# A hybrid decoder layer on one core: the opening takes two column chunks in turn, and its first loads come from two queues

## The chip, the core and the metric

The kernel runs on one core of a Trainium2 chip. TensorE (PE in the rows) multiplies, VectorE (DVE) and ScalarE (ACT) prepare operands and evacuate results, GpSimd (POOL) does a few tiny operations, and SyncE (SP) issues the loads, which the core's 16 DMA engines carry out. The metric is the device time of one execution in microseconds (us).

## The reference

One decoder layer on 256 tokens of width 1024, all in float32:

```
h = rms_norm(x, g_pre_mix);  proj = h @ w_in          # 1024 -> 3072: q, k, v of attention; q, k, v, gate of retention
x = x + rms_norm(concat(moba(...), retention(...)) @ w_out)
x = x + rms_norm(cross_attention(rms_norm(x), rms_norm(mem)) @ w_co)
x = x + rms_norm((silu(gate) * up) @ w_down)
```

## The kernel before

All weights come as one stream of 130 blocks of 128 x 1024 float32 (512 KB), in the order of use. A block q holds two k tiles (128 rows each) of 512 columns. `load_weight(q)` (line 120) issues its load from SyncE into one of five `raw` buffers, so the load of block q + 5 waits until block q has been split. `split_weight(q)` (line 125) splits it exactly into a high and a low part `hl` of type float32r: ScalarE copies the high part (line 131), VectorE subtracts to get the low part (line 132). `x`, transposed, is split in the same way into `xT`, one k tile (128 x 256) at a time, with the norm's gain multiplied in (`gain_split`, line 151: ScalarE line 154, VectorE line 155). A product of x and w is three passes: high x high, high x low, low x high. So a block costs TensorE 2 k tiles x 3 passes x 2 token tiles (`t`, 128 tokens each) = 12 matmuls of 512 columns.

TensorE's program is a list of steps, written once in Python (`steps`, `col_steps`, line 612). The first stage is the product with `w_in`, in six column chunks of 512; a chunk needs 4 blocks, one for each pair of k tiles, and accumulates in two PSUM banks, one per token tile. Between the steps, the Python code also emits the weight splits, a few blocks ahead, and the side work (rotation, attention, norms), which runs on the other engines and now and then puts small matmuls into TensorE's queue. The table `WAIT` holds by how many steps each part of the side work is delayed. Every engine runs its own queue strictly in the order in which the code emitted it.

The opening (from line 709): eight matmuls on zeros (`warm`, line 715), then the loads of x (`xg`: gains and k tile 0; `xr0`: k tiles 1 to 3; `xr1`: 4 to 7) and of blocks 0 to 4 (`raw0` in two halves of 256 KB), taken in turn, all from SyncE. Block 0 is taken half by half: the step `first` (line 817) goes over both token tiles in each of the three passes. From block 1 on the step `col` does all of token tile 0, and then token tile 1. Every loaded pair of k tiles of x has to be split on ScalarE and VectorE before the block that uses it.

```
for kk in range(2):
    steps.append(("first", 0, kk))
    steps.append(("none", 0))
for c in range(6):
    col_steps(plain([c]), both, in_done, "xT")
...
opening = {0: lambda: x_split(2), 1: lambda: x_split(3)}
late = {WAIT["xd"]: x_load, WAIT["xs"]: x_stats, WAIT["ms"]: mem_stats}
```

Of the kernel before, what the change touches and what calls it, by code (L numbers as in the profile page):

```python
# [14 lines left out]
P = 128  # L15
# [8 lines left out]
# main steps between the parts of the side work, and the pace of the weight splits  # L24
# [8 lines left out]
}  # L33
WARM = 8

# [4 lines left out]
def tile_hybrid_layer(  # L40
# [11 lines left out]
    """weights is one stream of 130 [128, 1024] blocks in the order of use.  Each float32 block is  # L52
    split exactly into hi + lo float32r parts; a product takes three float32r passes
    (hi*hi + hi*lo + lo*hi).  Tokens are the stationary operand, weights the moving one."""
# [53 lines left out]
    def need(*keys):  # L108
        """the producers of these parts have been emitted"""
        missing = [k for k in keys if k not in emitted]  # L110
        assert not missing, missing
# [56 lines left out]
    def row_rms(key):  # L168
        """1/rms of each token along the free axis, the same on all partitions."""
        T[f"R_{key}"] = cpool.tile([P, 256], F32, tag="R", name=f"R_{key}")  # L170
        c = accC(f"c_R_{key}")
        for t in range(2):
            nc.tensor.transpose(c[:, t, :], rstd[f"{key}{t}"][:, 0:1].to_broadcast([P, P]), ident)
        nc.scalar.activation(T[f"R_{key}"], c[:, 0:2, :].rearrange("p t k -> p (t k)"), AF.Copy)
# [44 lines left out]
    def softmax_unit(key, n, keys, scale, fill, row=None, finish=None):  # L219
        """fill(s) emits the scores of n heads into two banks; leaves the transposed probabilities in pt_key."""  # L220
# [41 lines left out]
    def moba_unit(t, g):  # L262
        keys = P * (t + 1)
        n = D // keys
        hn = n // 2

        def fill(s):
            """even heads in one bank, odd heads in the other; the contraction is over half of the rows"""
            need(f"q{t}", *[f"k{u}" for u in range(t + 1)])
            for i in range(hn):  # L270
                j = g * hn + i
                for e in range(2):
                    rows = slice(64 * e, 64 * e + 64)
                    nc.tensor.matmul(s[e][:, i * keys:(i + 1) * keys], T["qT"][rows, j, tok(t)],  # L274
                                     T["kT"][rows, j, 0:keys], start=(i == 0), stop=False, skip_group_check=True)
            for e in range(2):
                nc.tensor.matmul(s[e].rearrange("p (h k) -> p h k", h=hn)[:, :, keys - P:keys], identb,
                                 maskb[:, None, :].to_broadcast([P, hn, P]), start=False, stop=True,
                                 skip_group_check=True)
            yield 0  # L280

        return softmax_unit(f"m{t}{g}", n, keys, 0.125, fill)
# [46 lines left out]
    def ret_scores():  # L329
        """key block 0 against all queries, then key block 1 against query block 1"""  # L330
# [107 lines left out]
    def tri(dst, a, b, start, stop):  # L438
        """dst (+)= a.T @ b from the (hi, lo) parts of both"""
# [8 lines left out]
    def half_tiles(name):  # L448
        """[P, 8, 256] in two parts of four"""
# [163 lines left out]
    def col_steps(order, tiles, done, st):  # L613
        """order: list of (chunk, k pair); tiles: token tile order; one block of the stream each."""
# [6 lines left out]
        for i, t in seqs:  # L621
# [3 lines left out]
            if base + i == 0:  # L625
                continue
            steps.append(("col", base + i, t, st, kp, (c, t), s == 0, s + 1 == count[c], done))

    def row_steps(order, done, st):
        """like col_steps, but with the weights stationary: the result is transposed, two 128-wide  # L630
        column blocks of all 256 tokens per accumulator."""
# [16 lines left out]
    for kk in range(2):  # L648
        steps.append(("first", 0, kk))
        steps.append(("none", 0))  # L650
    for c in range(6):
# [58 lines left out]
    nc.vector.memset(junk[:, 0:512], 0.0)  # L710
    nc.gpsimd.memset(mhalf, -0.5)
    nc.scalar.preload_act_table(AF.Exp)
# [14 lines left out]
    raws[0] = rawp.tile([P, D], F32, tag="raw", name="raw0")  # L727
    for kk in range(2):
        nc.sync.dma_start(xg if kk == 0 else xr[0][:, 1, :], gx[:, 0:288] if kk == 0 else gx[:, 288:544])
        nc.sync.dma_start(raws[0][:, kk * 512:(kk + 1) * 512], weights[0, :, kk * 512:(kk + 1) * 512])  # L730
    for q in range(1, RAW):
        if q < 4:
            nc.sync.dma_start(xr[q // 2][:, 2 * (q % 2):2 * (q % 2) + 2, :],
                              gx[:, 32 + 512 * q:544 + 512 * q].rearrange("p (k m) -> p k m", k=2))
        load_weight(q)
# [48 lines left out]
    for kk in range(2):  # L784
        n = slice(kk * 512, (kk + 1) * 512)
        gain_split("xT", 0, xg[:, 32:288] if kk == 0 else xr[0][:, 1, :], kk)
        if kk == 0:
            nc.vector.tensor_copy(hls[0][:, 0, n], raw[:, n])
        else:
            nc.scalar.activation(hls[0][:, 0, n], raw[:, n], AF.Copy)  # L790
        nc.vector.tensor_tensor(out=hls[0][:, 1, n], in0=raw[:, n], in1=hls[0][:, 0, n].bitcast(F32), op=ALU.subtract)
    load_weight(RAW)
    x_split(1)
    split_weight(1, 2)
    opening = {0: lambda: x_split(2), 1: lambda: x_split(3)}
# [4 lines left out]
    for i, s in enumerate(steps):  # L800
# [17 lines left out]
        if s[0] == "first":  # L818
            kk = s[2]
            h = hls[0][:, :, kk * 512:(kk + 1) * 512]  # L820
            for a, (hx, hw) in enumerate(((0, 0), (1, 0), (0, 1))):
                for t in range(2):
                    if i == 0 and a == 0:
                        accs[(0, t)] = accS(f"acc{t}")
                    nc.tensor.matmul(accs[(0, t)], T["xT"][:, hx, kk, tok(t)], h[:, hw, :], start=(kk == 0 and a == 0),
# [77 lines left out]
def _layout(inputs):  # L903
# [11 lines left out]
    for c in (0, 1, 3, 4, 5, 2):  # L915
# [80 lines left out]
```

## Time and profile before

| | |
|---|---|
| median of 3 runs | 415.37 us (414.7 to 415.68) |
| profiled execution, first to last instruction | 415.7 us |
| mean granted TensorE clock in it | 0.994 of full speed |
| TensorE busy with matmuls | 405.9 us (98%), 2530 matmuls |
| VectorE / ScalarE / GpSimd busy | 261.0 / 219.8 / 11.0 us |
| bytes moved, mean rate | 76.23 MB, 183 GB/s |

The profiled execution's own time is its span, 415.7 us; the profile records nothing outside it. It lies 0.3 us above the median of the runs, and at the upper end of their range. Times in the rows are counted from the span's start. An engine is busy while an instruction of it runs; a wait is put down to what ended it.

### The profile page before, as it was taken

To read this page: it belongs to the slowest core of one execution; us is meant where nothing else is said; L and a number is where in the kernel's file an instruction comes from. 1 tells how busy PE (TensorE), PEld (TensorE's weight loads), DVE (VectorE), ACT (ScalarE), POOL (GpSimd) and SP (SyncE) were. 2 spreads that over 40 slices of the span, in tenths; PEclk is the share of its full clock that TensorE was granted. 3 is DMA by queue.
4 is the path that set the end of the run, shared out by engine and by line. 5 is a ranking of instruction groups with operands and counts; after the bars stand their busy time and mean duration, and the time that the engine had idled before them with its cause. 6 is when DMAs were issued, how large, how long until landed. Compare 5 with 4: busy or idle time off the path is not lost.

```text
span 415.7 us, 6402 instructions
## 1 busy us (share of the span) xinstructions
PE 405.9 (98%) x2530; PEld 359.6 (87%) x2530; DVE 261.0 (63%) x356; ACT 219.8 (53%) x360; POOL 11.0 (3%) x21
## 2 busy tenths in 40 slices
PE   6999999999999999999999999999999999999994
PEld 3788887888899999988888889989989989998983
DVE  4866875666848884576547867664674665566332
ACT  4956965945836673484346765352453443434111
POOL 0010010100010000000011000000000000000000
PEclk9899999999999999999999999999999999999999
DMA  7986846574645666135406777657447348353002
GB/s 247 417 322 215 297 131 224 151 247 155 190 169 178 224 248 213 52 101 202 153 0 203 239 246 271 207 188 211 160 158 245 122 145 291 106 203 102 0 21 82
DMA packets 21774, 76.23 MB, mean 183 GB/s; under 512 B 2416, under 2 KB 2672, under 8 KB 21744
## 3 DMA queue, kind: packets, MB, share of 16 engines
q1 hardware_dynamic: 21744, 75.82, 53.8%
q8 instruction: 20, 0.33, 0.3%
q14 instruction: 10, 0.08, 0.1%
HBM read 74.76 MB, written 1.05 MB: 182 GB/s over the span
## 4 chain that ended last, share of the span: by engine, by line
PE 94%; issue 2%; DMA 2%; SPq 1%; ACT 0%; DVE 0%; DVEq 0%; POOLq 0%; POOL 0%
PE acc L838 12%; PE acc L839 12%; PE acc L840 12%; PE acc L861 12%; PE acc L860 12%; PE acc L858 12%; PE down L881 4%; PE down L882 4%; PE down L880 4%; DMA raw<-in_weights_dram 2%; PE s_m L274 1%; PE o_m L303 1%; PE pt_m L253 1%; PE ro L356 0%; PE xt_cross L422 0%
## 5 line engine op out<-in xcount | busy, mean ns | idle before, releaser
L132 DVE TENSOR_TENSOR hl<-raw,hl 128x1024 fp32r<-128x1024 f32 (+1 forms) x132 | 154.1, 1198 | 49.4 <-ACT hl L131 49.1
L131 ACT ACTIVATE hl<-raw 128x1024 fp32r<-128x1024 f32 (+1 forms) x132 | 131.8, 1038 | 39.9 <-PE acc L861 15.0
L858 PE MATMUL acc<-x2T,hl 128*128 128x256 f32 x288 | 81.6, 283 | 0.0
L861 PE MATMUL acc<-x2T,hl 128*128 128x256 f32 x288 | 81.5, 283 | 0.0
L860 PE MATMUL acc<-x2T,hl 128*128 128x256 f32 x288 | 81.5, 283 | 0.0
L860 PEld LDWEIGHTS acc<-x2T,hl 128*128 128x128 f32 x288 | 55.3, 192 | 0.2
L858 PEld LDWEIGHTS acc<-x2T,hl 128*128 128x128 f32 x288 | 55.3, 192 | 0.2
L861 PEld LDWEIGHTS acc<-x2T,hl 128*128 128x128 f32 x288 | 55.3, 192 | 0.0
L838 PE MATMUL acc<-hl,xT 128*128 128x512 f32 x92 | 38.1, 414 | 1.7 <-ACT hl L131 1.7
L839 PE MATMUL acc<-hl,xT 128*128 128x512 f32 x92 | 36.6, 398 | 0.2 <-DVE hl L132 0.2
L840 PE MATMUL acc<-hl,xT 128*128 128x512 f32 x92 | 36.7, 399 | 0.0
L880 PE MATMUL down<-hl,fT 128*128 128x512 f32 x88 | 34.3, 390 | 0.0
L881 PE MATMUL down<-hl,fT 128*128 128x512 f32 x88 | 34.3, 390 | 0.0
L882 PE MATMUL down<-hl,fT 128*128 128x512 f32 x88 | 34.2, 389 | 0.0
L838 PEld LDWEIGHTS acc<-hl,xT 128*128 128x128 f32 x92 | 17.7, 193 | 5.8 <-ACT hl L131 2.1
L839 PEld LDWEIGHTS acc<-hl,xT 128*128 128x128 f32 x92 | 17.8, 193 | 3.8 <-DVE hl L132 0.5
L840 PEld LDWEIGHTS acc<-hl,xT 128*128 128x128 f32 x92 | 17.6, 191 | 3.8
L882 PEld LDWEIGHTS down<-hl,fT 128*128 128x128 f32 x88 | 16.5, 188 | 3.4
L880 PEld LDWEIGHTS down<-hl,fT 128*128 128x128 f32 x88 | 16.5, 188 | 3.3
L881 PEld LDWEIGHTS down<-hl,fT 128*128 128x128 f32 x88 | 16.5, 188 | 3.3
L510 ACT ACTIVATE sg<-sg 128x512 f32<-128x512 f32 x9 | 5.7, 633 | 24.9 <-DVE sg L509 24.9
L858 PE MATMUL acc<-memT,hl 128*128 128x256 f32 x64 | 18.4, 287 | 0.0
(207 smaller groups left out, 721.8 us busy)
## 6 DMA issues: line engine op xcount, KB each, us to landing
raw<-in_weights_dram SPq DMA_DIRECT2D x129, 512.0 KB, 4.4
gpost<-in_gpost_dram SPq DMA_DIRECT2D x3, 512.0 KB, 5.0
x_sb<-in_x_dram SPq DMA_DIRECT2D x2, 512.0 KB, 7.0
memn<-in_mem_dram SPq DMA_DIRECT2D x2, 512.0 KB, 6.1
mr<-in_memT_dram SPq DMA_DIRECT2D x2, 512.0 KB, 5.1
out_dram<-x_sb SPq DMA_DIRECT2D x4, 256.0 KB, 2.0
xr<-in_gx_dram SPq DMA_DIRECT2D x3, 256.0 KB, 6.5
raw<-in_weights_dram SPq DMA_DIRECT2D x2, 256.0 KB, 3.3
```

Of the source, the lines that this page charges most:

```text
L131: nc.scalar.activation(h[:, 0, n], raw[:, n], AF.Copy)
L132: nc.vector.tensor_tensor(out=h[:, 1, n], in0=raw[:, n], in1=h[:, 0, n].bitcast(F32), op=ALU.subtract)
L510: nc.scalar.activation(sg, sg, AF.Silu)
L838: nc.tensor.matmul(acc, xh, h[:, 0, kk, :], start=(first and kk == 0), stop=False)
L839: nc.tensor.matmul(acc, xh, h[:, 1, kk, :], start=False, stop=False)
L840: nc.tensor.matmul(acc, xl, h[:, 0, kk, :], start=False, stop=(last and kk == 1))
L858: nc.tensor.matmul(dst, h[:, 0, kk, n], xh, start=(first and b == 0 and kk == 0), stop=False, skip_group_check=True)
L860: nc.tensor.matmul(dst, h[:, 0, kk, n], xl, start=False, stop=False, skip_group_check=True)
L861: nc.tensor.matmul(dst, h[:, 1, kk, n], xh, start=False, stop=(last and kk == 1), skip_group_check=True)
L880: nc.tensor.matmul(acc, fh, wh, start=first, stop=False, skip_group_check=True)
L881: nc.tensor.matmul(acc, fh, wl, start=False, stop=False, skip_group_check=True)
L882: nc.tensor.matmul(acc, fl, wh, start=False, stop=last, skip_group_check=True)
```

## The change

1. The first two chunks of columns, 0 and 1, are taken in turn: for each pair of k tiles first the block of chunk 0, then that of chunk 1. The stream of weights is laid out in this order (blocks 0 to 7). Before, it was all four pairs for chunk 0, then all four for chunk 1.
2. Blocks 0 to 3 (`EARLY = 4`), not block 0 alone, use the step `first`, which goes over both token tiles in each pass. The accumulators of both chunks are then four banks of the pool `psS`.
3. The first half of block 0 is loaded from ScalarE's queue, ahead of its table load; the other loads stay on SyncE, without the strict alternation: block 1 is now ahead of k tiles 2 and 3, blocks 2 and 3 ahead of k tiles 4 to 7, which come as one load.
4. The splits of x stand later: those of k tiles 2 and 3 behind the split of block 1, those of 4, 5 and of 6, 7 behind the splits of blocks 4 and 6. For the first half of block 0 VectorE copies the weights before it makes the low part of x.
5. Five entries of `WAIT` change (`mq` from 2 to 0, `rope_q0` from 8 to 4, `rope_q1` from 9 to 5, `xd` from 0 to 3, `xs` from 8 to 12): the load of x in its natural layout, its statistics and the evacuation of the queries are emitted at other steps.

Comment lines that the change removes are left out here.

```
-    7, "rope_q0": 8, "rope_q1": 9, "rope_r0": 3, "rope_r1": 9, "rs": 1, "rsc": 12, "sc_c0": 0, "sc_c1": 1,
+    7, "rope_q0": 4, "rope_q1": 5, "rope_r0": 3, "rope_r1": 9, "rs": 1, "rsc": 12, "sc_c0": 0, "sc_c1": 1,
...
+EARLY = 4
...
-    for kk in range(2):
-        steps.append(("first", 0, kk))
-        steps.append(("none", 0))
-    for c in range(6):
+    early = [(c, kp) for kp in range(4) for c in (0, 1)]
+    for q in range(EARLY):
+        for kk in range(2):
+            steps.append(("first", q, kk, *early[q]))
+            if q == 0:
+                steps.append(("none", 0))
+    col_steps(early, both, in_done, "xT", EARLY)
+    for c in range(2, 6):
         col_steps(plain([c]), both, in_done, "xT")
...
+    raws[0] = rawp.tile([P, D], F32, tag="raw", name="raw0")
+    nc.scalar.dma_start(raws[0][:, 0:512], weights[0, :, 0:512])
     nc.scalar.preload_act_table(AF.Exp)
...
     load_weight(RAW)
+    split_weight(1, 2)
     x_split(1)
-    split_weight(1, 2)
-    opening = {0: lambda: x_split(2), 1: lambda: x_split(3)}
+    opening = {5: lambda: x_split(2), 8: lambda: x_split(3)}
...
         if s[0] == "first":
-            kk = s[2]
-            h = hls[0][:, :, kk * 512:(kk + 1) * 512]
+            _, q, kk, c, kp = s
+            h = hls[q][:, :, kk * 512:(kk + 1) * 512]
             for a, (hx, hw) in enumerate(((0, 0), (1, 0), (0, 1))):
                 for t in range(2):
...
-                    nc.tensor.matmul(accs[(0, t)], T["xT"][:, hx, kk, tok(t)], h[:, hw, :], start=(kk == 0 and a == 0),
+                    nc.tensor.matmul(accs[(c, t)], T["xT"][:, hx, 2 * kp + kk, tok(t)], h[:, hw, :], start=begin,
                                      stop=False)
...
-    for c in (0, 1, 3, 4, 5, 2):
+    for kp in k4:
+        for c in (0, 1):
+            blocks += cols(w_in, c * 512, (kp,))
+    for c in (3, 4, 5, 2):
         blocks += cols(w_in, c * 512, k4)
```

Three places of the engines' queues show what moves; a row is a line of the code, an operation, and output <- inputs with the shape (the number behind a name is that of a buffer). First SyncE's queue from the program's start, before:

```order
L729 DMA xg_94<-in_gx_dram 128x288
L730 DMA raw0_119<-in_weights_dram 128x512
L729 DMA xr0_117<-in_gx_dram 128x256
L730 DMA raw0_119<-in_weights_dram 128x512
L733 DMA xr0_117<-in_gx_dram 128x512
L123 DMA raw1_125<-in_weights_dram 128x1024
L733 DMA xr1_118<-in_gx_dram 128x512
L123 DMA raw2_128<-in_weights_dram 128x1024
```

and the same place after:

```order
L735 DMA xg_94<-in_gx_dram 128x288
L736 DMA raw0_102<-in_weights_dram 128x512
L737 DMA xr0_119<-in_gx_dram 128x256
L125 DMA raw1_124<-in_weights_dram 128x1024
L739 DMA xr0_119<-in_gx_dram 128x512
L125 DMA raw2_127<-in_weights_dram 128x1024
L125 DMA raw3_129<-in_weights_dram 128x1024
L742 DMA xr1_120<-in_gx_dram 128x1024
```

Block 1 (`raw1`) moves from the sixth place to the fourth, with the second half of block 0 in the second place; the first half is gone from this queue.

Second, ScalarE's queue at the start, before:

```order
L154 ACTIVATE xT_115<-xg_94 128x256
L154 ACTIVATE xT_115<-xr0_117,xg_94 128x256
L790 ACTIVATE hl0_135<-raw0_119 128x512
L154 ACTIVATE xT_115<-xr0_117,xg_94 128x256 x2
L131 ACTIVATE hl1_150<-raw1_125 128x512 x2
L154 ACTIVATE xT_115<-xr1_118,xg_94 128x256 x2
L131 ACTIVATE hl2_172<-raw2_128 128x512 x2
```

and after:

```order
L719 DMA raw0_102<-in_weights_dram 128x512
L720 ACT_TABLE_LOAD
L156 ACTIVATE xT_117<-xg_94 128x256
L156 ACTIVATE xT_117<-xr0_119,xg_94 128x256
L798 ACTIVATE hl0_134<-raw0_102 128x512
L133 ACTIVATE hl1_145<-raw1_124 128x512 x2
L156 ACTIVATE xT_117<-xr0_119,xg_94 128x256 x2
L133 ACTIVATE hl2_164<-raw2_127 128x512 x2
L133 ACTIVATE hl3_177<-raw3_129 128x512 x2
L133 ACTIVATE hl4_195<-raw4_132 128x1024
L156 ACTIVATE xT_117<-xr1_120,xg_94 128x256 x2
```

The split of block 1 no longer has the two splits of `xr0` in front of it, and VectorE's queue moves in the same way.

Third, ScalarE's queue where chunks 0 and 1 are evacuated (`nat_q0`, `nat_q1`: queries of the two token tiles; `nat_k0`, `nat_k1`: keys), before:

```order
L149 ACTIVATE junk_98,ss_x1_249<-x_sb_95 128x1024
L131 ACTIVATE hl7_261<-raw7_177 128x1024
L166 ACTIVATE nat_q0_273<-acc0_157,r_x0_247 128x512
L166 ACTIVATE nat_q1_287<-acc1_159,r_x1_253 128x512
L131 ACTIVATE hl8_294<-raw8_194 128x1024
L131 ACTIVATE hl9_311<-raw9_205 128x1024
L131 ACTIVATE hl10_322<-raw10_222 128x1024
L166 ACTIVATE nat_k0_339<-acc10_266,r_x0_247 128x512
```

and after:

```order
L151 ACTIVATE junk_98,ss_x1_284<-x_sb_95 128x1024
L133 ACTIVATE hl9_296<-raw9_198 128x1024
L168 ACTIVATE nat_q0_307<-acc00_156,r_x0_282 128x512
L133 ACTIVATE hl10_314<-raw10_219 128x1024
L168 ACTIVATE nat_q1_325<-acc01_158,r_x1_288 128x512
L168 ACTIVATE nat_k0_338<-acc10_187,r_x0_282 128x512
```

The queries are evacuated two to three blocks later, close before the keys. TensorE's own queue has the same 2381 rows in the same order of operations and shapes, before and after; only the lines and the buffers differ.

## Rows read from the trace of the kernel before

**Rows 1.** Waits of TensorE, whole span: engine line waited for: total us, times, longest.
```profile
PE acc L838 <- ACT hl L131: 1.7, 1, 1.7
...
PE acc L825 <- ACT hl L790: 0.6, 1, 0.6
PE acc L839 <- DVE hl L132: 0.2, 1, 0.2
```

**Rows 2.** Stages (us): busy time (count) per engine, granted clock, DMA share, GB/s.
```profile
4.45:6.10 1.65, 1.64 (x7) 1.04 (x6) 1.05 (x2) 0.55 (x2) 0.00 (x0) 1.00 1.01 237
...
10.10:14.40 4.30, 4.07 (x10) 3.01 (x11) 4.30 (x9) 4.28 (x9) 0.00 (x0) 0.61 1.03 415
```

**Rows 3.** TensorE by time: start, us, line, op, shape, count [idle before].
```profile
1.19 3.38 PE L715 MATMUL warm<-junk 128*128 128x512 bf16 x8 [1.19 <-DVE junk L710]
4.47 1.62 PE L825 MATMUL acc<-hl,xT 128*128 128x512 f32 x6
6.74 1.66 PE L825 MATMUL acc<-hl,xT 128*128 128x512 f32 x6 [0.65 <-ACT hl L790]
10.07 0.50 PE L838 MATMUL acc<-hl,xT 128*128 128x512 f32 x1 [1.67 <-ACT hl L131]
10.80 0.61 PE L839 MATMUL acc<-hl,xT 128*128 128x512 f32 x1 [0.23 <-DVE hl L132]
11.21 0.63 PE L840 MATMUL acc<-hl,xT 128*128 128x512 f32 x1
...
14.78 0.39 PE L840 MATMUL acc<-hl,xT 128*128 128x512 f32 x1
15.01 0.39 PE L838 MATMUL acc<-hl,xT 128*128 128x512 f32 x1
...
34.55 0.60 PE L215 MATMUL c_k<-cst,nat_k 128*128 128x128 f32 x4
```

**Rows 4.** ScalarE by time; in brackets the idle time before, and what ended it.
```profile
2.96 0.51 ACT L154 ACTIVATE xT<-xg 128x256 fp32r<-128x256 f32 x1 [0.94 <-DMA xg<-in_gx_dram]
5.10 0.51 ACT L154 ACTIVATE xT<-xr,xg 128x256 fp32r<-128x256 f32 x1 [1.64 <-DMA xr<-in_gx_dram]
6.06 0.63 ACT L790 ACTIVATE hl<-raw 128x512 fp32r<-128x512 f32 x1 [0.44 <-DMA raw<-in_weights_dram]
7.85 0.91 ACT L154 ACTIVATE xT<-xr,xg 128x256 fp32r<-128x256 f32 x2 [1.16 <-DMA xr<-in_gx_dram]
9.39 1.15 ACT L131 ACTIVATE hl<-raw 128x512 fp32r<-128x512 f32 x2 [0.63 <-DMA raw<-in_weights_dram]
...
15.87 1.06 ACT L131 ACTIVATE hl<-raw 128x1024 fp32r<-128x1024 f32 x1 [0.21 <-DMA raw<-in_weights_dram]
...
22.60 1.25 ACT L166 ACTIVATE nat_q<-acc,r_x 128x512 f32<-128x512 f32 x2
```

**Rows 5.** VectorE by time, the opening and the turn of the keys.
```profile
3.90 0.42 DVE L788 CAST hl<-raw 128x512 fp32r<-128x512 f32 x1
...
6.72 0.69 DVE L791 TENSOR_TENSOR hl<-raw,hl 128x512 fp32r<-128x512 f32 x1 [0.59 <-ACT hl L790]
8.40 0.88 DVE L155 SCALAR_TENSOR_TENSOR xT<-xr,xg,xT 128x256 fp32r<-128x256 f32 x2 [0.98 <-ACT xT L154]
...
30.92 0.23 DVE L206 TENSOR_TENSOR rt_k<-nat_k,cst 128x64 f32<-128x64 f32 x1 [1.97 <-ACT nat_k L166]
...
31.52 0.29 DVE L211 TENSOR_TENSOR nat_k<-rt_k 128x128 f32<-128x128 f32 x1
31.87 1.23 DVE L132 TENSOR_TENSOR hl<-raw,hl 128x1024 fp32r<-128x1024 f32 x1
```

**Rows 6.** SyncE's load issues by time, first and eighth.
```profile
0.74 0.38 SPq L729 DMA_DIRECT2D xg<-in_gx_dram  x1
...
4.01 0.62 SPq L123 DMA_DIRECT2D raw<-in_weights_dram  x1
```

**Rows 7.** Loads issued between 3.7 and 4.3 us: KB, us from issue to landing.
```profile
raw<-in_weights_dram SPq DMA_DIRECT2D x1, 512.0 KB, 7.3
```

More of the change, by code (lines that the diff above doesn't have):

```diff
@@ L611, in tile_hybrid_layer, with col_steps @@
     nq = [0]
-    def col_steps(order, tiles, done, st):
+    def col_steps(order, tiles, done, st, skip=0):
         count, seen = {}, {}
@@ L624, in col_steps @@
             seen[(c, t)] = s + 1
-            if base + i == 0:
+            if i < skip:
                 continue
@@ L726, in tile_hybrid_layer @@
     xr = [p4.tile([P, 4, 256], F32, tag="p4", name=f"xr{i}") for i in range(2)]
[L727 to L735, printed above, removed]
+    nc.sync.dma_start(xg, gx[:, 0:288])
+    nc.sync.dma_start(raws[0][:, 512:1024], weights[0, :, 512:1024])
+    nc.sync.dma_start(xr[0][:, 1, :], gx[:, 288:544])
+    load_weight(1)
+    nc.sync.dma_start(xr[0][:, 2:4, :], gx[:, 544:1056].rearrange("p (k m) -> p k m", k=2))
+    load_weight(2)
+    load_weight(3)
+    nc.sync.dma_start(xr[1], gx[:, 1056:2080].rearrange("p (k m) -> p k m", k=4))
+    load_weight(4)
     def x_split(kp):
@@ L785, in tile_hybrid_layer @@
         n = slice(kk * 512, (kk + 1) * 512)
-        gain_split("xT", 0, xg[:, 32:288] if kk == 0 else xr[0][:, 1, :], kk)
         if kk == 0:
             nc.vector.tensor_copy(hls[0][:, 0, n], raw[:, n])
-        else:
+        gain_split("xT", 0, xg[:, 32:288] if kk == 0 else xr[0][:, 1, :], kk)
+        if kk == 1:
             nc.scalar.activation(hls[0][:, 0, n], raw[:, n], AF.Copy)
@@ L818, in tile_hybrid_layer @@
         if s[0] == "first":
-            kk = s[2]
-            h = hls[0][:, :, kk * 512:(kk + 1) * 512]
+            _, q, kk, c, kp = s
+            h = hls[q][:, :, kk * 512:(kk + 1) * 512]
             for a, (hx, hw) in enumerate(((0, 0), (1, 0), (0, 1))):
                 for t in range(2):
-                    if i == 0 and a == 0:
-                        accs[(0, t)] = accS(f"acc{t}")
-                    nc.tensor.matmul(accs[(0, t)], T["xT"][:, hx, kk, tok(t)], h[:, hw, :], start=(kk == 0 and a == 0),
+                    begin = kp == 0 and kk == 0 and a == 0
+                    if begin:
+                        accs[(c, t)] = accS(f"acc{c}{t}")
+                    nc.tensor.matmul(accs[(c, t)], T["xT"][:, hx, 2 * kp + kk, tok(t)], h[:, hw, :], start=begin,
                                      stop=False)
```

6 rows, old and new, of the table WAIT are left out of this document.

## The prediction

> **What bounds the kernel now.** I began with the list of what TensorE waited for over the whole span [rows 1]. Three waits for data stand there, 1.7, 0.6 and 0.2 us, and no other: once the third has ended, at 10.80 us, TensorE is never again without work until its last product. The time of the kernel is therefore the moment at which this unbroken stream starts, plus its length, and only the opening can be shortened. Next the stages [rows 2]: from 10.1 to 14.4 us the granted clock averaged 0.61, so TensorE ran there mostly at the lower of its two levels (1.2 and 2.4 GHz), and it fell behind the longest wait. TensorE by time [rows 3] gives the sizes: the two halves of block 0 start at 4.47 and 6.74 us, block 1 at 10.07 us; a matmul follows the one before after 0.41 us at 10.80 and after 0.23 us from 14.78 on. The matmul at 15.01 us is the 25th of the opening, so two blocks have cost 15.01 - 4.47 = 10.5 us, where 24 x 0.23 = 5.5 us of work stand in them. At most 5.0 us can be won: 2.5 of waits, about 1.7 by the clock (4.30 us at a mean of 0.61), the rest restarts.
>
> What the waits wait for stands in ScalarE's rows [rows 4]: each piece starts when its load lands. SyncE issues a load each 0.47 us ((4.01 - 0.74)/7 [rows 6]), and in the order of issue the sum of KB and the landing are: 528 (up to k tile 1) at 5.10, 784 (block 0) at 6.06, 1040 (k tiles 2, 3) at 7.85, 1552 (block 1) at 9.39 [rows 4], 2320 (block 2) at 4.01 + 7.3 = 11.3 us [rows 6, 7]. The opening is bound by these bytes: a load lands when what was issued ahead of it has passed.
>
> **The work of TensorE.** The change leaves count, shape and order of all its matmuls as they are. The term is 0; what counts is when the stream becomes unbroken.
>
> **The first matmul.** The eight matmuls on zeros run from 1.19 us for 3.38 us, up to the first real one [rows 3]. An earlier first half of block 0 gains nothing there: 0. It is issued up to 0.43 us earlier but shares the engines with `xg`; in the trace VectorE's copy starts at 3.90 and takes 0.42 us [rows 5], and has 0.15 us to spare. At worst this costs a few tenths, which the next gate hides. ScalarE's issue ahead of its table load takes perhaps 0.4 us, as one of SyncE's does, and falls into the 0.94 us in which it waited for `xg` anyway [rows 4].
>
> **The second queue.** From 4.45 to 6.10 us the DMA engines were taken to a share of 1.01 at 237 GB/s [rows 2], with one queue. So a second queue can bring an earlier start, not more bytes. I take 0.3 us for all landings, between 0 and the 0.43 to 0.47 us of one issue. The Trainium skill says the same (DMA: Bandwidth & Descriptors, "Issuing engines are not separate DMA queues"): whichever engine starts them, transfers run on the same 16 engines, and several issuers save only the time to initiate; the trace agrees. By it the sum below stands; if the queue had bandwidth of its own, the 256 KB would leave the sum, block 1 would land about 0.8 us earlier, and the gain would be near 4.
>
> **Second half of block 0.** Ahead of it and of k tile 1 now stand 784 KB together, with k tile 1 last, which lands at 6.06 - 0.3 = 5.8 us (before: 5.10). ScalarE then needs 0.51 for the high part of x and 0.63 for that of the weights [rows 4]: TensorE starts at 6.9 us against 6.74, and ends block 0 at 8.6 (1.66 us [rows 3]) against 8.4. A loss of 0.2, which the next gate hides too.
>
> **Block 1: the term that decides.** It now stands behind 784 KB and not behind 1040: with its own 512, 1296 KB. Between 1040 at 7.85 and 1552 at 9.39, that is 8.6; less 0.3, 8.3 us. ScalarE needs half of 1.15 us for the first half [rows 4], so TensorE starts block 1 at 8.9 us instead of 10.07, and the wait ahead of it falls from 1.7 to about 0.3 us. The low parts follow in time: VectorE takes 0.69 us a half [rows 5], so the first is there at 9.6, and the two passes over both token tiles that don't need it last till 8.9 + 4 x 0.23 = 9.8. That is what going over both tiles per pass is worth: the 0.23 us wait [rows 1] goes. Twelve matmuls at 0.23 end at 11.7 us, if the clock stays up.
>
> **Block 2 and on.** The next thing late would be k tiles 2 and 3 (1552 KB: 9.4 - 0.3 = 9.1 us, two splits of together 0.91 behind block 1's, done at 10.4) and block 2 (2064 KB, 10.7 - 0.3 = 10.4, high part at 11.0). TensorE comes at 11.7: 0.7 us of cover. Block 3 is for the same k tiles, so one pair of x now feeds two blocks, 5.5 us of work, and bytes arrive at 415 GB/s [rows 2], a block in 1.3 us against 2.7 us that TensorE takes for it. For block 4 the split of k tiles 4, 5 stands behind that of block 4, on ScalarE and VectorE: it lands (3600 KB) by about 14.2, 1.06 us and 0.91 us later [rows 4] the high parts are there, at 16.2, the first low part at 16.9 (VectorE's 1.23 and half of 0.88 [rows 5]); TensorE needs them from 11.7 + 2 x 2.7 = 17.1. Cover again, 0.5 us or more. I see no new wait.
>
> **The turn of the keys.** The queries are evacuated later, ahead of the keys, in ScalarE's and VectorE's queue. Before, the keys were rotated at 31.81 (31.52 + 0.29 [rows 5]) and transposed by TensorE at 34.55 [rows 3]: 2.7 us of cover. Now TensorE comes 3.3 earlier, at 31.2. Block 9 lands (7472 KB in all, at 415 GB/s from the 2320) at about 23.7; then 1.06 for its split, 0.6 + 1.06 + 0.6 + 0.6 for queries, block 10 and keys [rows 4] on ScalarE, and on VectorE 1.2, 0.9, 1.2, 0.9 and 0.9 (splits of 1.23 and rotations from 30.92 to 31.81 [rows 5]): 23.7 + 1.1 + 5.1 = 29.9. Cover of 1.3 us, so 0.
>
> **The sum.** The 25th matmul starts at 11.7 instead of 15.01: 3.3 us less. Against the profiled execution's own 415.7 us that is 412.4; the median of the runs lies 0.3 lower, 415.37, and I forecast against it: 415.4 - 3.3 = 412.1. The bounds of the earlier start (0 and 0.47) give 411.9 to 412.4, and with 0.2 us for reading landings between rows this case has 411.7 to 412.6. Changes under 0.2%, 0.8 us, can't be told from none.
>
> **Rivals.**
> - *The clock falls all the same.* In the trace it stood at the upper level up to the long wait and fell after waits of 0.6 and 1.7 us in 5.6 us [rows 1, 2]; now about 0.8 (6.1 to 6.9) and 0.3 remain. For it: waits there still are. Against: half the idle time, and between 4.47 and 8.4 us a wait of 0.6 did not bring it down. Price: the 1.7 us of the row at 0.61, so a gain of 1.6 and 413.8. The Trainium skill (TensorE: Matmul & The Clock Gate, "HAM oscillation — how this bites in real kernels") tells of kernels whose matmuls wait for loads between bursts and start each burst at the lower clock again. By that rule it is this rival; the trace shows the fall once, after the longest wait. Chance 0.15.
> - *Block 1 lands no earlier,* since what is queued behind it takes the engines' time and its order among the issues does not count. Against: the landings follow the order of issue in every row. Then TensorE starts at about 10.0, gains 2.2 at the upper clock (413.2) and 0.5 with the fall (414.9). Chance 0.12, a third of it the second.
> - *No wait at all:* bytes come faster, since the many 1 and 2 KB rows of x now stand behind block 1. Gain 4.1 to 5.0, 410.4 to 411.3. Chance 0.09.
> - *Slower: the side work catches TensorE.* If x in its natural layout and block 9 came so late (they are issued behind block 8 now) that the rotated keys were ready more than 3.3 us after TensorE comes for them, the kernel would be slower: landings 4.6 us later than worked out give everything back, 5.4 us later make it 416.2, 5.7 us 416.5. The engines' queue is never empty in that stretch, so only a much lower rate would do it. Chance 0.06.
>
> My forecast keeps 0.58. The likeliest case and the first three rivals lie between 410.4 and 414.4 but for the part of the second that keeps the old start, and a fall deeper than priced: about 0.87 inside. Faster by over 0.2%: 0.58 + 0.09 + most of 0.15 and two thirds of 0.12, 0.86; within it 0.09, slower 0.05.
>
> **What would show it.** Right: TensorE's waits in the opening add up to 1.2 us or less, the one ahead of block 1 ends between 8.5 and 9.3 us, the granted clock from 8.4 to 14.4 us is 1.00, and 0.23 us a matmul from block 1 on. Wrong: a mean clock under 0.9 there; block 1's split starting after 9 us; a wait at block 2, at block 4 or at the keys' transposes; or anything moved after 36 us, where the queues are the same.

## The result and the profile after

| | before | after |
|---|---|---|
| median (9 runs each) | 415.68 us | 413.86 us |
| lowest, highest | 414.7, 417.48 | 413.18, 414.15 |
| ratio after / before, 95% interval | | 0.9941 [0.9924, 0.9959] |
| profiled execution, span | 415.7 us | 411.4 us |

The change makes the kernel 0.6% faster, 1.8 us, and the interval leaves 1 out; 412.1 had been forecast. The device time of a run is its span plus 1.7 to 1.9 us in every execution whose span is known: the profiled execution after, with its 411.4, took 413.18. By this the trace of before, with its span of 415.7, belongs to an execution of about 417.5 us, not to one of 415.4, and lies not 0.3 but about 2 us above the median. This matters below.

The list of what TensorE waited for holds, after, only the wait for the zeros at the start; the three waits for data of [rows 1] are gone:

```profile
PE warm L723 <- DVE junk L716: 1.2, 1, 1.2
```

TensorE by time (as [rows 3]), the opening and the first transposes of queries and keys:

```profile
1.19 3.60 PE L723 MATMUL warm<-junk 128*128 128x512 bf16 x8 [1.19 <-DVE junk L716]
4.79 11.40 PE L835 MATMUL acc<-hl,xT 128*128 128x512 f32 x47
...
10.81 0.39 PE L835 MATMUL acc<-hl,xT 128*128 128x512 f32 x1
...
28.50 0.60 PE L217 MATMUL c_q<-cst,nat_q 128*128 128x128 f32 x4
...
30.33 0.60 PE L217 MATMUL c_k<-cst,nat_k 128*128 128x128 f32 x4
```

From 4.79 us on the four blocks of `first` run through, in one row that merges 47 matmuls. The row at 10.81, from a narrower stretch, is the 25th of them; [rows 3] has the 25th at 15.01, so it comes 4.2 us earlier. The keys' transposes start at 30.33, before at 34.55: again 4.2 earlier, and that is nearly the whole gain between the two traces (415.7 - 411.4 = 4.3). The stages of [rows 2], same columns:

```profile
4.45:6.10 1.65, 1.65 (x7) 0.98 (x6) 1.28 (x4) 0.70 (x3) 0.00 (x0) 1.00 0.91 305
6.10:8.40 2.30, 2.18 (x10) 1.52 (x9) 1.67 (x3) 1.64 (x4) 0.00 (x0) 1.00 1.03 397
...
10.10:14.40 4.30, 4.30 (x20) 3.56 (x20) 2.59 (x5) 2.77 (x5) 0.00 (x0) 1.00 1.03 416
```

The clock from 10.1 to 14.4 us is 1.00 (0.61 in [rows 2]), and from 4.45 to 6.10 the engines moved 305 GB/s, at a smaller busy share (0.91) than before with 237 (1.01). These two rates say nothing of the change: in the second traces (experiments 1 and 2) it is 323 GB/s before, at a share of 0.95, and 259 after, at 0.91. ScalarE by time, as [rows 4]:

```profile
4.04 0.51 ACT L156 ACTIVATE xT<-xg 128x256 fp32r<-128x256 f32 x1 [1.59 <-DMA xg<-in_gx_dram]
5.51 0.51 ACT L156 ACTIVATE xT<-xr,xg 128x256 fp32r<-128x256 f32 x1 [0.95 <-DMA xr<-in_gx_dram]
5.92 0.61 ACT L798 ACTIVATE hl<-raw 128x512 fp32r<-128x512 f32 x1
7.20 1.15 ACT L133 ACTIVATE hl<-raw 128x512 fp32r<-128x512 f32 x2 [0.66 <-DMA raw<-in_weights_dram]
8.25 0.90 ACT L156 ACTIVATE xT<-xr,xg 128x256 fp32r<-128x256 f32 x2
9.43 2.41 ACT L133 ACTIVATE hl<-raw 128x512 fp32r<-128x512 f32 x4 [0.28 <-DMA raw<-in_weights_dram]
```

`xg` landed 1.1 us later (4.04 for 2.96) and k tile 1 0.4 later (5.51 for 5.10); the blocks, for which TensorE had waited, landed earlier: block 1 at 7.20 for 9.39, block 2 by 9.43 for 11.3.

### The profile page after: what moved, and what is told of

Its sections match the earlier page's. It is cut to its first block, busy times and chain, and to the rows that moved or that the text cites. A ratio compares the mean times of both kernels' runs of the same rounds, so it can differ in the third digit from the quotient of the medians.

```text
span 411.4 us, 6399 instructions
## 1 busy us (share of the span) xinstructions
PE 404.0 (98%) x2530; PEld 358.6 (87%) x2530; DVE 260.5 (63%) x356; ACT 219.0 (53%) x360; POOL 11.0 (3%) x21
## 3 DMA queue, kind: packets, MB, share of 16 engines
HBM read 74.76 MB, written 1.05 MB: 184 GB/s over the span
## 4 chain that ended last, share of the span: by engine, by line
PE 95%; issue 2%; DMA 1%; ACT 1%; DVE 0%; SPq 0%; DVEq 0%; POOLq 0%; POOL 0%
PE acc L871 12%; PE acc L868 12%; PE acc L870 12%; PE acc L848 12%; PE acc L850 12%; PE acc L849 12%; PE down L890 4%; PE down L892 4%; PE down L891 4%; PE acc L835 2%; DMA xr<-in_gx_dram 1%; PE s_m L276 1%; PE o_m L305 1%; PE pt_m L255 1%; PE ro L358 0%
## 5 line engine op out<-in xcount | busy, mean ns | idle before, releaser
L848 PE MATMUL acc<-hl,xT 128*128 128x512 f32 x80 | 32.7, 409 | 0.0
L850 PE MATMUL acc<-hl,xT 128*128 128x512 f32 x80 | 31.3, 392 | 0.0
L849 PE MATMUL acc<-hl,xT 128*128 128x512 f32 x80 | 31.2, 390 | 0.0
L868 PE MATMUL acc<-memT,hl 128*128 128x256 f32 x64 | 18.4, 287 | 0.0
L870 PE MATMUL acc<-x1T,hl 128*128 128x256 f32 x64 | 18.1, 283 | 0.0
L871 PE MATMUL acc<-memT,hl 128*128 128x256 f32 x64 | 18.1, 283 | 0.0
L868 PE MATMUL acc<-x1T,hl 128*128 128x256 f32 x64 | 18.1, 283 | 0.0
```

Of the source, the lines that this page charges most:

```text
L848: nc.tensor.matmul(acc, xh, h[:, 0, kk, :], start=(first and kk == 0), stop=False)
L849: nc.tensor.matmul(acc, xh, h[:, 1, kk, :], start=False, stop=False)
L850: nc.tensor.matmul(acc, xl, h[:, 0, kk, :], start=False, stop=(last and kk == 1))
L868: nc.tensor.matmul(dst, h[:, 0, kk, n], xh, start=(first and b == 0 and kk == 0), stop=False, skip_group_check=True)
L870: nc.tensor.matmul(dst, h[:, 0, kk, n], xl, start=False, stop=False, skip_group_check=True)
L871: nc.tensor.matmul(dst, h[:, 1, kk, n], xh, start=False, stop=(last and kk == 1), skip_group_check=True)
```

## The experiments

Edits are against the kernel after where nothing else is said. The kernel before ran beside them; its medians are 415.91 (35 runs, beside 1 to 4), 415.92 (24, beside 5 to 8) and 416.85 us (17, beside 9 to 11). Its runs fall into two groups of times (experiment 1), so these medians, and the ratios to them, also depend on how many runs of each group were drawn. The lower group alone has medians of 415.64, 415.79 and 415.47 us, so a difference of 0.3 us or less between experiments of different sets shows nothing.

**1. The kernel before, again.** No edit.

> The kernel before, once more, for the span and the clock of every run. Theory A (the clock of the opening is drawn anew in each execution): most runs have a mean clock of about 0.998 and a span near 413.9 us, that is the 415.7 of the profile before less the 1.7 us that the lower clock cost there; a few have 0.994 and 415.7. Theory B (what is shown in the one trace is what every execution does): all runs have 0.994 and a span of 415.4 to 415.9.

415.87 us (415.16 to 417.8, 12 runs). Its profiled execution (415.16 us, span 413.4), TensorE by time:

```profile
4.48 1.83 PE L825 MATMUL acc<-hl,xT 128*128 128x512 f32 x6
6.93 1.66 PE L825 MATMUL acc<-hl,xT 128*128 128x512 f32 x6 [0.62 <-ACT hl L790]
9.46 0.50 PE L838 MATMUL acc<-hl,xT 128*128 128x512 f32 x1 [0.87 <-ACT hl L131]
10.19 0.50 PE L839 MATMUL acc<-hl,xT 128*128 128x512 f32 x1 [0.22 <-DVE hl L132]
10.52 0.39 PE L840 MATMUL acc<-hl,xT 128*128 128x512 f32 x1
10.75 0.39 PE L838 MATMUL acc<-hl,xT 128*128 128x512 f32 x1
...
12.80 0.39 PE L838 MATMUL acc<-hl,xT 128*128 128x512 f32 x1
```

And the stage behind it, by windows as [rows 2]:

```profile
10.10:14.40 4.30, 4.21 (x19) 3.49 (x20) 4.30 (x10) 4.13 (x9) 0.00 (x0) 1.00 1.04 422
```

The same three waits stand there, together 1.7 us and not 2.5, but no fall of the clock: 1.00 where [rows 2] has 0.61, and 0.23 us a matmul from 10.52 on, where [rows 3] has 0.41. The row at 12.80 is its 25th matmul. Theory A holds. The spans differ by 2.3 us (415.7 - 413.4): 0.6 by the later start of block 1 (10.07 - 9.46), and the 1.7 that the fall had been priced at. All 88 runs of this kernel in these comparisons form two groups with nothing between 416.18 and 416.79: 54 runs with a median of 415.64 (mean clock 0.995 to 0.999) and 34 with 417.48 (0.993 to 0.995), from here on the lower and the upper group. They are 1.84 us apart. The trace that the prediction read has the time and the clock of the upper group; that its 34 runs have the fall in the opening too is read from their time and clock alone.

**2. The kernel after, again.** No edit.

> The changed kernel, once more. Theory A: spans of 411.4 to 412.4 with a mean clock of 0.995 to 0.998, and no run with a fall in the opening, since no wait is left; a second trace shows the same unbroken stream from 4.8 us. Theory B: 411.4 in nearly all. If a trace has a span near 412.1 and waits in the opening that the first trace did not have, the 0.7 us between typical runs and the trace are landings that come later, not the clock.

413.78 us (413.13 to 414.73, 12 runs), 0.9947 [0.9929, 0.9966]. Its trace has one wait, ahead of block 1, which was split at 7.73:

```profile
4.64 3.18 PE L835 MATMUL acc<-hl,xT 128*128 128x512 f32 x12
8.42 3.94 PE L835 MATMUL acc<-hl,xT 128*128 128x512 f32 x16 [0.60 <-ACT hl L133]
```

So that wait stands in one execution and not in another, as the last sentence of the expectation has it; "the same unbroken stream" was not found. In 21 runs of the kernel after none was above 414.73: none stands out as a fall would. Against the lower group of before the gain is 415.64 - 413.8 = 1.8 us, against the upper 3.7.

**3. One queue.** The first half of block 0 goes back to SyncE, the order of loads stays.

```
-    nc.scalar.dma_start(raws[0][:, 0:512], weights[0, :, 0:512])
...
     nc.sync.dma_start(xg, gx[:, 0:288])
+    nc.sync.dma_start(raws[0][:, 0:512], weights[0, :, 0:512])
```

> The changed kernel with the first half of block 0 issued from SyncE, behind the first load of x, as before; all else as changed. Theory 1 (the second queue only shares the engines, and delays the first load of x): the first load of x lands at 3.0 us instead of 4.0, the first matmul starts at 4.5 instead of 4.8, and the time is 0.3 us less than the changed kernel's. Theory 2 (the second queue brings the bytes earlier): block 1 lands 0.4 us or more later than 7.2, waits of 0.3 us or more come back ahead of it, and the time is 0.3 us more.

414.24 us (12 runs), 0.996 [0.9943, 0.9976], 0.46 slower than with both queues (experiment 2, beside it), as theory 2 has it. The first matmul starts earlier (4.35, `xg` at 2.95), the rest lands later; its waits:

```profile
PE acc L835 <- ACT hl L798: 0.4, 1, 0.4
PE acc L835 <- ACT hl L133: 0.2, 1, 0.2
```

And ScalarE by time:

```profile
2.95 0.51 ACT L156 ACTIVATE xT<-xg 128x256 fp32r<-128x256 f32 x1 [0.94 <-DMA xg<-in_gx_dram]
...
8.03 1.15 ACT L133 ACTIVATE hl<-raw 128x512 fp32r<-128x512 f32 x2 [1.24 <-DMA raw<-in_weights_dram]
```

**4. The loads of before.** Also the order of the loads of before; what stays of the change is the order of the work.

```
+    for kk in range(2):
+        nc.sync.dma_start(xg if kk == 0 else xr[0][:, 1, :], gx[:, 0:288] if kk == 0 else gx[:, 288:544])
+        nc.sync.dma_start(raws[0][:, kk * 512:(kk + 1) * 512], weights[0, :, kk * 512:(kk + 1) * 512])
+    for q in range(1, RAW):
...
```

> The changed kernel with all the first loads as in the kernel before (one queue, x and weights strictly in turn); the two chunks in turn, both token tiles per pass and the order of the splits stay. Theory L (the order of the loads wins, since block 1 stands behind fewer bytes): block 1 lands at about 9.4 us again, TensorE starts it at 10.0, and of the gain at most 0.5 us is left against the kernel before. Theory I (taking the chunks in turn wins, since one pair of x feeds two blocks): at least 1.5 us of the gain are left.

415.37 us (414.69 to 417.03, 12 runs), 0.9984 [0.9965, 1.0004]: what is left of the gain can't be told from none, and block 1's split starts at 9.51 again, as theory L has it. The trace is of a run of 416.42, 1.05 above the median. TensorE's waits in it:

```profile
PE acc L833 <- ACT hl L133: 1.3, 1, 1.3
...
PE c_k L217 <- DVE nat_k L213: 0.8, 1, 0.8
PE acc L833 <- ACT hl L796: 0.5, 1, 0.5
```

The wait at `c_k`, for the rotated keys, is the mechanism of the "slower" rival: in this run block 9 was split at 27.56 (after: 22.92), and the keys came later than TensorE. Whether the typical runs have it isn't known. With the new loads it is hidden. By steps, from the lower group's 415.64: order of the work 0.3, not told from none; order of the loads 1.1 (experiment 3 against this one); second queue 0.5. The steps hang on each other: with the new loads one part of the order of the work, both token tiles per pass, is worth about 0.5 by itself (experiment 6).

**5. The waits filled.** Against the kernel before: in the empty steps of the opening stand 2 and 5 matmuls on zeros.

```
+        elif s[0] == "none":
+            for _ in range(2 if i == 1 else 5):
+                nc.tensor.matmul(warm, junk[:, 0:P], junk[:, 0:512], start=True, stop=True)
```

> The kernel before, with matmuls on zeros put into TensorE's queue where it waits: two (0.2 us each) between the halves of block 0, five ahead of block 1. Loads, splits and all other work stay; the waits are filled, not shortened. Theory A (the lower clock follows the waits): the runs near 417.5 us, about a third of the kernel before, are gone; all lie between 414 and 416.4 and the median is 415.5 to 415.9. Rival (the clock falls for a reason outside the matmul stream): a quarter or more of the runs are still above 417 us.

415.71 us, all 12 runs from 415.02 to 416.14; beside it 9 of 24 runs of before were above 417. The useful work starts no earlier (block 1 at 9.92), and what goes is the upper group of times, as theory A has it. That filling the idle time removes the group is shown. It is not the sum of the idle time alone: experiment 7 keeps waits of 1.6 us, and none of its 12 runs is in the upper group. What decides it in a given execution isn't shown either: experiment 9 has a longer wait than any of before in its trace, with the clock at 1.00 behind it.

**6. Block 0 alone over both token tiles** (`EARLY = 1`; the two chunks in turn and the loads stay).

```
-EARLY = 4
+EARLY = 1
```

> The changed kernel with EARLY = 1: blocks 1 to 3 take all of token tile 0 and then tile 1, as before; the rest as changed. If going over both tiles per pass is worth the 0.23 us wait for the low part of the weights that the kernel before has ahead of the second matmul of block 1, that wait comes back and the time is 0.2 us more than the changed kernel's in the same call, 414.0. Rival: the start is bound by the landing of block 1 alone, and the time is the same within 0.1. Second rival: the low parts of x come late too at blocks 2 and 3, and it is 0.5 us or more.

414.48 us (7 runs), 0.9953 [0.9936, 0.9971], 0.6 to 0.7 slower than after, which was measured apart. The 0.2 us wait of [rows 1] is back. TensorE's waits, and TensorE by time:

```profile
PE acc L848 <- ACT hl L133: 0.4, 1, 0.4
PE acc L849 <- DVE hl L134: 0.2, 1, 0.2
```

```profile
8.93 0.50 PE L848 MATMUL acc<-hl,xT 128*128 128x512 f32 x1 [0.42 <-ACT hl L133]
9.66 0.50 PE L849 MATMUL acc<-hl,xT 128*128 128x512 f32 x1 [0.22 <-DVE hl L134]
10.00 0.40 PE L850 MATMUL acc<-hl,xT 128*128 128x512 f32 x1
```

The wait costs more than its 0.2 us, since the list counts it from the modelled end of the matmul before, 0.50 after that one's start: from start to start it is 0.73 (8.93 to 9.66) and then 0.34, where the others follow after 0.23, together 0.6 more. From block 1's start to the keys' transposes this trace takes 22.87 us (31.80 - 8.93), that of experiment 2 22.38 (30.80 - 8.42): 0.5 more. So the step itself costs about 0.5 us, which is most of the 0.6 to 0.7; the second rival has the size, the first theory the mechanism. That block 1 was also split later in this trace (8.25) makes up the rest of the 1.0 between the two spans (412.9 and 411.9).

**7. The second queue alone.** Against the kernel before: only the first half of block 0 is issued by ScalarE.

```
+    nc.scalar.dma_start(raws[0][:, 0:512], weights[0, :, 0:512])
     nc.scalar.preload_act_table(AF.Exp)
...
-        nc.sync.dma_start(raws[0][:, kk * 512:(kk + 1) * 512], weights[0, :, kk * 512:(kk + 1) * 512])
+        if kk:
+            nc.sync.dma_start(raws[0][:, 512:1024], weights[0, :, 512:1024])
```

> The kernel before with one edit: the first half of block 0 is issued from ScalarE's queue ahead of its table load; all other loads keep their order on SyncE, now one place earlier. If the second queue saves one issue for all that follow, block 1 starts 0.4 us earlier and the typical run is 0.3 to 0.5 us shorter (415.4). Rival (it delays the first load of x to 4.0 us, the first matmul to 4.8 and gains nothing after): the same or up to 0.3 us more. The share of runs near 417.5 should stay about a third, since the waits stay.

414.98 us (12 runs), 0.9967 [0.9951, 0.9982]: 0.8 us under the lower group of before beside it (415.79), more than the 0.3 to 0.5 expected. None of the 12 runs is above 415.65, where a third had been expected near 417.5: that was a miss, with waits of 1.1, 0.3 and 0.2 us still in the trace. TensorE by time:

```profile
5.65 2.99 PE L827 MATMUL acc<-hl,xT 128*128 128x512 f32 x12 [1.15 <-DVE hl L790]
8.93 0.50 PE L840 MATMUL acc<-hl,xT 128*128 128x512 f32 x1 [0.30 <-ACT hl L131]
```

Block 0 starts 1.2 later, yet block 1 0.5 earlier than in experiment 1. VectorE by time says why the start is late:

```profile
4.68 0.48 DVE L155 SCALAR_TENSOR_TENSOR xT<-xg,xT 128x256 fp32r<-128x256 f32 x1 [3.55 <-ACT xT L154]
5.08 0.42 DVE L790 CAST hl<-raw 128x512 fp32r<-128x512 f32 x1
```

It copies the weights, for which TensorE waits, behind the low part of x; part 4 of the change puts the copy first (at 4.21 in the trace after).

**8. Block 1 on the second queue too.**

```
+    raws[1] = rawp.tile([P, D], F32, tag="raw", name="raw1")
+    nc.scalar.dma_start(raws[1], weights[1])
...
-    load_weight(1)
...
```

> The changed kernel with block 1, too, issued from ScalarE's queue, right behind the first half of block 0. If the bytes bind, it shares the engines with the first load of x and the second half of block 0, these land later, the first matmul starts 0.3 us or more after 4.8, and the time is the same or more (413.8 to 414.5). Rival (the order in one queue still holds block 1 back): it lands before 7.2 us in each run, the wait of up to 0.6 us ahead of it goes, and the time is 413.2 to 413.4.

414.34 us (6 runs), about 0.5 slower than after, measured apart; the first expectation has the time, though the first matmul hardly moved (4.85). The DMA engines moved more (398 GB/s from 4.5 to 6.5 us; after 315, and 277 in experiment 2), but k tile 1, needed first, landed at 6.63 for 5.51, and TensorE waited 1.1 us between the halves of block 0.

**9. A load that nothing reads.** Experiment 3, with 256 KB more on ScalarE's queue.

```
+    extra = pt4.tile([P, D], F32, tag="pt4", name="extra")
+    nc.scalar.dma_start(extra[:, 0:512], weights[0, :, 0:512])
```

> The changed kernel with all of its first loads on SyncE (as in e3), and an extra load of 256 KB that nothing reads, issued from ScalarE's queue ahead of its table load. Theory R (in the opening one queue alone does not fill the DMA engines; with both at work more bytes move per us): from 3.0 to 4.5 us the rate is above 370 GB/s against 290 in e3, and block 1 lands at most 0.3 us later than there in spite of 256 KB more. Theory S (a second queue saves only an issue; the rate is what it is): block 1 lands 0.6 to 0.9 us later (8.6 to 8.9), and the median is 0.6 us or more above e3's 414.2.

415.0 us (12 runs), 0.8 slower than experiment 3, measured apart. The runs are spread: six from 414.46 to 414.76, four from 415.24 to 415.68, and two at 417.77 and 418.07, so that an upper group isn't ruled out here. The trace is of the run of 415.68. The rate rises as in the other kernels with two queues (410 GB/s from 3.0 to 4.5 us), so it doesn't depend on what is loaded. The rate is as theory R has it and the median as theory S has it; in this trace the landing misses both: block 1's split starts at 9.60, 1.6 later than in experiment 3. ScalarE by time, and below it TensorE's longest wait and the stage behind it:

```profile
7.93 0.51 ACT L156 ACTIVATE xT<-xr,xg 128x256 fp32r<-128x256 f32 x1 [3.28 <-DMA xr<-in_gx_dram]
8.34 0.61 ACT L800 ACTIVATE hl<-raw 128x512 fp32r<-128x512 f32 x1
9.60 1.15 ACT L133 ACTIVATE hl<-raw 128x512 fp32r<-128x512 f32 x2 [0.64 <-DMA raw<-in_weights_dram]
```

```profile
PE acc L837 <- ACT hl L800: 1.8, 1, 1.8
```

```profile
10.10:14.40 4.30, 4.30 (x21) 3.53 (x20) 4.14 (x8) 3.76 (x8) 0.00 (x0) 1.00 1.02 412
```

By windows, everything up to the start of block 1's split, in experiment 3 and then here:

```profile
0.00:8.03 8.03, 6.41 (x19) 3.47 (x20) 2.87 (x6) 2.82 (x5) 0.31 (x5) 1.00 0.71 221
0.00:9.60 9.60, 5.82 (x17) 2.51 (x18) 2.79 (x6) 2.82 (x5) 0.31 (x5) 1.00 0.79 275
```

That is 1.77 MB and 2.64 MB (rate times length). Block 1, what SyncE issued ahead of it and the extra load are 1.33 MB there (1296 KB) and 1.59 MB here (1552 KB). So 0.45 and 1.05 MB that had moved by then belonged to loads issued behind block 1: before a load has landed, bytes of later ones have moved, here far more of them.

**10. Both halves of block 0 on the second queue.**

```
     nc.scalar.dma_start(raws[0][:, 0:512], weights[0, :, 0:512])
+    nc.scalar.dma_start(raws[0][:, 512:1024], weights[0, :, 512:1024])
...
-    nc.sync.dma_start(raws[0][:, 512:1024], weights[0, :, 512:1024])
```

> The changed kernel with both halves of block 0 on ScalarE's queue, and x and block 1 on SyncE's. Theory R: both queues stay at work longer, block 1 lands at 7.2 us or before, the second half of block 0 by 5.3, no wait is left in the opening but the first matmul's start at about 4.8, and the time is 413.2 to 413.5. Theory S: landings as in the changed kernel, time 413.6 to 414.

413.5 us (6 runs), 0.9931 [0.9907, 0.9955]. No wait in its trace, and the time is theory R's; block 1's landing isn't (its split starts at 7.62, for 7.2 or before).

**11. x on the second queue.** `xg` and k tile 1 go on ScalarE's queue, both halves of block 0 and block 1 on SyncE's.

```
-    nc.scalar.dma_start(raws[0][:, 0:512], weights[0, :, 0:512])
+    nc.scalar.dma_start(xg, gx[:, 0:288])
...
+    nc.scalar.dma_start(xr[0][:, 1, :], gx[:, 288:544])
...
-    nc.sync.dma_start(xg, gx[:, 0:288])
+    nc.sync.dma_start(raws[0][:, 0:512], weights[0, :, 0:512])
...
-    nc.sync.dma_start(xr[0][:, 1, :], gx[:, 288:544])
```

> The changed kernel with k tiles 0 and 1 of x on ScalarE's queue and block 0 and block 1 on SyncE's: the queues split by what is loaded, 272 KB on the second one. Theory R: the rate from 3.0 to 4.5 us is as in the changed kernel, block 1 lands at about 7.4, and the time is that of the changed kernel or up to 0.3 us less. Theory S, by which only the number of issues ahead counts: block 1 is now the third issue on SyncE and not the fourth, so it lands 0.4 us earlier than in the changed kernel and the time is 413.3.

413.33 us (412.97 to 413.84, 6 runs), 0.9929 [0.9907, 0.9951]: the lowest median of the study, 0.5 below that of after, though the two were measured apart (against the lower group of before beside each, 2.1 us and 1.9). No wait in its trace, and block 1's split starts at 6.32, earlier than either theory had it, so the landing doesn't tell them apart. ScalarE by time:

```profile
6.32 1.15 ACT L133 ACTIVATE hl<-raw 128x512 fp32r<-128x512 f32 x2 [0.21 <-DMA raw<-in_weights_dram]
```

The rates of all these, GB/s by stretch (the last column of the view by windows), and the bytes that follow from them (rate times length, summed):

| kernel, profiled execution | 1.5 to 3.0 | 3.0 to 4.5 | 4.5 to 6.5 | 6.5 to 8.0 us | MB |
|---|---|---|---|---|---|
| before (first trace) | 231 | 266 | 254 | 291 | 1.69 |
| 3: one queue, new order | 236 | 285 | 276 | 292 | 1.77 |
| 4: one queue, old order | 251 | 250 | 224 | 320 | 1.68 |
| after | 167 | 388 | 315 | 401 | 2.06 |
| 9: one queue and an extra load | 146 | 410 | 329 | 359 | 2.03 |
| 11: x on the second queue | 172 | 392 | 385 | 427 | 2.26 |

Over all thirteen traces the two kinds are apart in three of the four stretches: one queue (5 traces) 212 to 251, 250 to 285 and 291 to 320 GB/s, two queues (8 traces) 146 to 172, 384 to 410 and 337 to 427. From 4.5 to 6.5 us they overlap (224 to 330 and 266 to 398).

## Why the prediction was right and where it was wrong

**The time: inside the range partly by luck.** 413.86 lies outside 411.7 to 412.6, the span of the sum, and inside 410.4 to 414.4, which the rivals opened. It is nearly the figure of the rival "the clock falls all the same" (413.8), but no such fall came: two misses of opposite sign, given below, led there. Of the signs that were named for "right", the opening's waits (0 and 0.6 us), the clock (1.00 from 8.4 to 14.4 us in both traces) and the pace of 0.23 us came true; block 1 started earlier than the 8.5 to 9.3 given, at 8.07 and 8.42.

**What bounds the kernel, and the chain behind it: right.** Only the opening moved; what follows is the same stream, started earlier, and no new wait came. At the keys a cover of 1.3 us was worked out: the keys were rotated at 28.88 + 0.29 = 29.17, TensorE came at 30.33, cover 1.16. The row is VectorE's, as [rows 5]:

```profile
28.88 0.29 DVE L213 TENSOR_TENSOR nat_k<-rt_k 128x128 f32<-128x128 f32 x1
```

**The base: wrong, and the largest miss.** "Against the profiled execution's own 415.7 us that is 412.4; the median of the runs lies 0.3 lower" took the span for the time of a run. The time is 1.8 more, so the trace was of an execution of the upper group, and its 1.7 us of low clock, counted into the "5.0 us that can be won", are not to be won in the 54 of 88 runs of the lower one, if those all go as experiment 1's trace does. On its own base the same sum is 417.5 - 3.3 = 414.2, which is 0.4 from the 413.8 measured. Against experiment 1's trace, whose 25th matmul starts at 12.80, the forecast start of 11.7 gains 1.1, and from 415.64 that gives 414.5.

**Block 1's landing: the order counts, but the rule was too simple and the size off.** Taken: landing at 8.3 us, and a wait of 0.3. Measured: 7.20 and no wait in one execution, 7.73 and 0.60 in the other. That the order of issue counts is shown by experiment 3 against 4 (8.03 for 9.51, 1.1 us of time). But "a load lands when what was issued ahead of it has passed" is not what the bytes say: by the start of block 1's split 0.60 MB more than block 1 and all ahead of it had moved in the trace of before (9.39 us at a mean of 233 GB/s, less 1552 KB), 0.42 in that of after (7.20 us at 242, less 1296 KB), 0.45 and 1.05 in experiments 3 and 9. That fits the second rival's mechanism, that what is queued behind takes the engines' time, but also a landing that is seen some time after the load's last byte; the rows don't tell the two apart. Between the trace of before and that of after the gain was 4.3, not 3.3: the rival "no wait at all" (4.1 to 5.0) is what the trace shows, but from a higher base. So the base made the forecast 2.1 us too low, and the gain, 0.4 too small (against the 3.7 between the medians of the upper group and of after), made it 0.4 too high: together 1.7 to 1.8 too low.

**The second queue: mis-sized.** "A second queue can bring an earlier start, not more bytes", 0.3 us. It was worth 0.46 (experiment 3 against 2) and 0.8 (7 against the lower group of before), and it brought bytes: from 3.0 to 4.5 us 250 to 285 GB/s with one queue and 384 to 410 with two. The argument from [rows 2] failed because a busy share of 1.01 at 237 GB/s isn't a bound: in its second row 1.03 goes with 415 GB/s, and in experiment 1 the same stretch of the same kernel has 323 GB/s at 0.95. The Trainium skill (DMA: Bandwidth & Descriptors, "Issuing engines are not separate DMA queues") says that issuing from several engines saves only the time to initiate the DMA. The prediction says that the trace agrees, but a trace with one queue can't show it; the traces with two disagree, by these rates. Nor did the queue give its load a bandwidth of its own: experiments 8 and 9 show that the loads on SyncE's queue land later for it.

**The first matmul: not 0, but a loss of 0.2 to 0.3.** 4.79 and 4.64 for 4.47, with `xg` 1.1 us later; it had been said that the copy has 0.15 to spare, and the copy started at 4.21 for 3.90. The next gate hid it, as said. The second half of block 0 had been put at 6.9 and started at 6.59 in the trace after.

**Going over both token tiles: right in kind, too small.** 0.2 had been taken for the wait that goes; experiment 6 makes the step worth about 0.5, since a wait in the list is shorter than the time lost from start to start.

**The clock falls all the same** (chance 0.15): in neither trace of after, and none of its 21 runs has a time that would go with it. Filling the waits of before took the upper group away too. The Trainium skill (TensorE: Matmul & The Clock Gate, "HAM oscillation — how this bites in real kernels") tells of a kernel that starts at the lower clock after every wait for loads, its waits being longer than these. The trace of before agrees in kind, with one fall; experiment 1, the same kernel, has waits and no fall.

**Open:** why two queues move more, and go on to do so after the second queue's 256 KB are in (401 GB/s after and 427 in experiment 11 from 6.5 to 8.0 us); why in experiment 9 so many more bytes of later loads passed ahead of block 1 (1.05 MB for 0.45); and what decides on the fall in one execution.

## What to carry to other kernels

Before a sum is made against a trace, find out which of the kernel's executions it shows: set its span plus the fixed part of a run against the spread of the runs, and look at the clock by stage. In an opening that is bound by loads, try issuing from two queues, but in the order in which the pieces are needed: that was worth 0.5 to 0.8 us here, while more bytes a second, of pieces not needed first, were slower (experiments 8, 9). A rate at a busy share of 1.0 of the DMA engines was not yet their limit (237 GB/s at 1.01, 415 at 1.03). And the cost of a wait is read from the starts of the matmuls around it, not from its length alone (experiment 6: 0.2 us in the list, 0.5 in time).

## What the runs showed of the hardware that was not expected

- The same kernel has two times, medians 415.64 and 417.48 us, with no run between 416.18 and 416.79; the two traces of it, one of each, differ in the clock after the waits of the opening (1.00 and 0.61). With the waits filled the upper group was gone (experiment 5).
- Two queues move fewer bytes at first (146 to 172 GB/s from 1.5 to 3.0 us, one queue 212 to 251) and more from 3.0 to 4.5 us (384 to 410, one queue 250 to 285); the first load of x is about 1 us later for it (ScalarE starts on it at 3.86 to 4.14, with one queue at 2.95 to 3.08), on whichever of the two queues it stands (experiment 11: 4.05).
- When block 1 had landed, 0.42 to 1.05 MB of loads issued behind it had moved too (traces of before, after, experiments 3 and 9).
